# Reading the up projection's weight tiles with a step of 1, 2, 4 and 8 columns

## The chip, the cores and the metric

The kernel runs on one core of a Trainium2 chip. The metric is the time on the device in microseconds (us) of one execution; the times shown are medians of several runs. TensorE (PE in the profile) multiplies matrices: a weight load (PEld) puts the stationary operand, up to 128x128, into the array, and a matmul then streams the moving operand through it, column by column, into a bank of PSUM. VectorE (DVE), ScalarE (ACT) and the DMA queues of SyncE (SP) prepare operands beside it.

## What is computed

Two transformer blocks over 256 tokens with 2048 features, one after the other: the first with a gated linear recurrence, the second with three branches (pooling, convolution, sparse attention) and an MLP. The change touches the first product of that MLP only:

```python
h = rmsnorm(x, g[2])
m = jnp.square(jax.nn.relu(h @ w_up[l])) @ w_down[l]
x = x + rmsnorm(m, g[3])
```

`w_up` is 2048 x 8192, `w_down` is 8192 x 2048, all in fp32.

## The kernel before

Every fp32 product is made of three products of parts: an operand is split into a high part (rounded to the matrix unit's fp32r) and a low part (the rest), and high x high, high x low and low x high are summed in PSUM.

Weights come as a stream of chunks of 128 x 2048 numbers (1 MB), in the order of their use, built in the list `chunks`. `_pack` on the host lays them out; `_kchunks` makes of the matrix chunks that hold, for four blocks of 128 input rows, four tiles of 128 columns each, tile behind tile. `Stream.load` (L59) transfers a chunk into one of three buffers `wraw` on SyncE's queue. A chunk is split in two pieces of 1024 columns: `split_hi` (L87, ScalarE) writes the high part `whi`, `split_lo` (L98, VectorE) writes the low part `wlo` and, when the piece is the chunk's last, issues the next transfer. There are five buffers each of `whi` and `wlo`, so the split runs ahead of the matmuls.

The MLP is worked in four quarters, `q` = 0 to 3 (L1558). In each, the up projection computes 2048 of the 8192 hidden features for all 256 tokens: four groups of four output tiles (`Wide(4)`, one PSUM bank for each tile), each over 16 blocks of input features; then the down projection takes these 2048 features in (`Tok`, lines L409 to L411, where the weights are the moving operand). `full` (L453) calls `linear` for four chunks in turn, and `linear` (L430) takes a split piece and issues for each of its eight tiles the matmuls of `Wide.mac`: the tile of `whi` as stationary operand against 512 moving columns (high and low parts of 256 tokens, L376), and the tile of `wlo` against 256 moving columns (the high parts, L377). That makes 4 x 16 x 4 = 256 pairs of matmuls in a quarter, each matmul with a weight load of its own. After each piece `pumped` issues the next split and whatever vector or scalar work is due. The moving operand is `N`, the split and normalised input of the MLP, which stays in SBUF for all quarters. The tile of `whi` that a matmul takes is 128 columns that stand next to each other.

Of the kernel before, what the change touches and what calls it, by code (L numbers as in the profile page):

```python
# [23 lines left out]
P = 128  # L24
T = 256
D = 2048
KT = D // P
# [14 lines left out]
    _NV += _w  # L42

_POOL_FIX = 16
_ATT_GROUPS = 5


class Stream:
# [159 lines left out]
def tile_kernel(ctx: ExitStack, tc: tile.TileContext, d):  # L208
# [213 lines left out]
    def pumped(tiles):  # L422
        l = ws.split_lo()
        h = ws.split_hi()
        us = tiles * 0.3275
        S.pump(us, ACT=0.95 * h, DVE=1.13 * l, PE=us - 0.7)

    def linear(grp, kts, rhs, pieces, last_kt, before=None):

        kts = list(kts)  # L430
        per = len(kts) // pieces
        for p in range(pieces):
            hi, lo = ws.take()
            for a in range(per):
                kt = kts[p * per + a]
                x = rhs(kt)
                if isinstance(grp, Tok):
                    c = slice(a * 512, (a + 1) * 512)
                    for t in range(2):
                        grp.mac(t, hi[:, c], lo[:, c], *x[:2], kt == last_kt)  # L440
                    continue
                if isinstance(grp, Wide):
                    x = (x[2],)
                else:
                    x = x[:2]
                for m in range(grp.n):
                    c = (a * grp.n + m) * P
                    grp.mac(m, hi[:, c:c + P], lo[:, c:c + P], *x, kt == last_kt)
            if before is not None:
                before(kts[p * per])  # L450
            pumped(per * grp.n)

    def full(grp, rhs, n=KT):  # L453
        for c in range(n // 4):
            linear(grp, range(4 * c, 4 * c + 4), rhs, 2, n - 1)

    def full_by_bank(grp, rhs, evac, n=KT):

# [20 lines left out]
    def hl16(n):  # L479
        return sb.tile([P, 2, KT, T], F32R, tag="B32", bufs=2, name=n)  # L480
# [314 lines left out]
    for m in range(4):  # L795
        grp = Group(4)
# [14 lines left out]
        grp = Group(4)  # L811
# [20 lines left out]
    def out_last(rhs, fill=(None, None), idle=(0, 0)):  # L832

        grp = Group(4)
        sq = []

        def evac(b):
            if b == 0:
                sq.append(t4(n="sq"))
            act.activation(sq[0][:, 2 * b:2 * b + 2, :], grp.banks[b], AF.Square)  # L840
            if b == 0:
                norm.fold2(sq[0])

        full_by_bank(grp, rhs, evac)
        pumped(8)
        if fill[0]:
            fill[0]()
        t = norm.rstd(extra=[sq[0][:, 2, :], sq[0][:, 3, :]],
                      fill=(lambda: pumped(8), fill[1]) if fill[1] else (), idle=idle)
        S.free(T4=1)  # L850
        return grp, t
# [27 lines left out]
    def proj(n, half=None):  # L879
        if n not in pgrp:  # L880
            pgrp[n] = (Group(4), ws.take())
        grp, (hi, lo) = pgrp[n]
        for k in (0, 1) if half is None else (half,):
            for m in range(4):
                c = (4 * k + m) * P
                grp.mac(m, hi[:, c:c + P], lo[:, c:c + P], ph[:, k, :], pl[:, k, :], k == 1)
# [13 lines left out]
    g, r_copy = out_last(rhsY, fill=(lambda: proj(0, 0), lambda: proj(0, 1)))  # L900
# [55 lines left out]
    for n in range(4):  # L956
        g = Wide(4)
# [55 lines left out]
    for c in range(4):  # L1013
        for p in range(2):
            hi, lo = ws.take()
# [241 lines left out]
    for n in range(2):  # L1257
        g = Group(4)
# [71 lines left out]
    for m in range(8):  # L1330
        g = Group(3)
# [113 lines left out]
    for n in range(4):  # L1445
        if n == 3:
            A(1.28, lambda: table(AF.Sqrt))
            g, r_copy = out_last(rhsM, idle=(3, 7))
            break
        g = Wide(4)  # L1450
# [39 lines left out]
    rhsN = rhs_of(N, n_ready)  # L1490
# [67 lines left out]
    for q in range(4):  # L1558
        HD = hl16(f"HD{q}")
        ready = {}  # L1560
        for n in range(4):
            g = Wide(4)
            full(g, rhsN)
            if r4_done[0] is None:
                A(1.28, lambda: table(AF.Sqrt))
                r4_done[0] = norm.rstd(wait=False)
            up_done(n, g, HD, ready)
        if q == 0:
            for n in range(4):
                turn(n)  # L1570
        if q == 2:
            gains_ready.append(A(0.1, load_gains, take=T4[2]))
        rh = rhs_of(HD, ready)
        for n in range(4):
            if q == 3 and n == 3:
                break
            g = Tok()
            full(g, rh)
            down_done(q, n, g)
# [3 lines left out]
    g = Tok()  # L1583
# [24 lines left out]
    for t in range(2):  # L1608
        for a in range(4):
            hi, lo = hl[a // 2]  # L1610
            c = slice(a % 2 * 512, (a % 2 + 1) * 512)
# [6 lines left out]
def _kchunks(w, groups, kper=4):  # L1618

    k = w.shape[0] // P  # L1620
    out = []
    for cols in groups:
        a = np.concatenate([w[:, c:c + P] for c in cols], axis=1)
        a = a.reshape(k // kper, kper, P, len(cols) * P).transpose(0, 2, 1, 3)
        out.append(a.reshape(k // kper, P, kper * len(cols) * P))
    return np.ascontiguousarray(np.concatenate(out, axis=0))


def _fours(m, base=0):
    return [[base + (4 * g + i) * P for i in range(4)] for g in range(m // (4 * P))]  # L1630

# [7 lines left out]
def _cols(v):  # L1639
    return v.reshape(-1, P).T  # L1640
# [9 lines left out]
def _pack(i):  # L1650
    a = {}
    x, pe_ = i["x"][0], i["p"][0, 0]
    a["xT"] = _featT(x)
    a["pT"] = _featT(pe_)
    g = i["norm_gains_2"][0]
    vecs = [i["norm_pre"][0], i["norm_post"][0], i["a_conv_w"][0].reshape(-1), i["a_conv_b"][0],
            i["a_b_r"][0].reshape(-1), i["a_b_i"][0].reshape(-1), i["a_lam"][0], g[0], g[1], g[2], g[3],
            i["pool_scale_2"][0], i["conv_w_2"][0].reshape(-1)]
    a["vec"] = np.ascontiguousarray(np.concatenate([_cols(v) for v in vecs], axis=1))

    w = i["a_w_in"][0]
    order = []
    for m in range(4):
        order += [[(4 * m + t) * P for t in range(4)], [D + (4 * m + t) * P for t in range(4)]]
    a["a_in"] = _kchunks(w, order)
    ri = np.concatenate([i["a_w_r"][0], i["a_w_i"][0]], axis=2)
    ri = ri.reshape(4, 2, 2, P, 512).transpose(0, 3, 1, 2, 4)
    a["a_ri"] = np.ascontiguousarray(ri.reshape(4, P, 2048))
    a["a_out"] = _kchunks(i["a_w_out"][0], _fours(D))
    w = i["ple_w_proj"][0].reshape(2, P, 2, 2, 512).transpose(2, 1, 3, 0, 4)  # L1670
    a["ple_proj"] = np.ascontiguousarray(w.reshape(2, P, 2048))
    a["ple_gate"] = _kchunks(i["ple_w_gate"][0], _fours(D))

    w = i["w_in_2"][0]
    o_pool, o_u, o_c, o_b, o_q, o_k, o_v, o_qi, o_ki, o_wi = np.cumsum(
        [0, 1024, 1024, 1024, 1024, 1024, 256, 256, 1024, 64]).tolist()
    ki2 = np.concatenate([w[:, o_ki:o_ki + 64]] * 2, axis=1)
    att = np.concatenate([ki2, w[:, o_qi:o_qi + 1024], w[:, o_k:o_k + 256], w[:, o_q:o_q + 1024]], axis=1)
    a["att"] = _kchunks(att, _fours(2048))
    a["att3"] = _kchunks(att, [[16 * P, 17 * P, 18 * P]])  # L1680
    vw = np.concatenate([w[:, o_v:o_v + 256], w[:, o_wi:o_wi + 16]], axis=1)
    vw = vw.reshape(4, 4, P, 272).transpose(0, 2, 1, 3)
    a["vwi"] = np.ascontiguousarray(vw.reshape(4, P, 4 * 272))
    a["pool_in"] = _kchunks(w, _fours(1024, o_pool))
    pw = i["pool_w_2"][0].reshape(4, 2, P, 256).transpose(2, 0, 1, 3)
    a["pool_w"] = np.ascontiguousarray(pw.reshape(1, P, 2048))
    a["conv_in"] = _kchunks(w, [[o_u + m * P, o_c + m * P, o_b + m * P] for m in range(8)])
    a["gate"] = _kchunks(i["w_gate_2"][0], _fours(3 * D))
    a["branch"] = np.concatenate([_kchunks(i["w_branch_2"][0, n], _fours(D)) for n in range(3)])
    a["w_out"] = _kchunks(i["w_out_2"][0], _fours(D))  # L1690
    a["up"] = _kchunks(i["w_up_2"][0], _fours(4 * D))
    w = i["w_down_2"][0]
    a["down"] = np.concatenate([_kchunks(w[q * D:(q + 1) * D], _fours(D)) for q in range(4)])

    t = np.arange(_POOL_FIX)
    fix = np.concatenate([w_ / np.minimum(t + 1, w_) for w_ in (2, 4, 8, 16)])
    tri = np.where(np.arange(P)[None, :] <= np.arange(P)[:, None], 0.0, FLT_MASKED)
    a["cst"] = np.concatenate([np.broadcast_to(fix, (P, 4 * _POOL_FIX)), np.eye(P), tri],
                              axis=1).astype(np.float32)
    rel = i["rel_bias_2"][_bucket(P + np.arange(P)[:, None] - np.arange(T)[None, :])]  # L1700
    a["rel"] = np.ascontiguousarray(rel.reshape(P, T, 2, 4).transpose(2, 0, 3, 1))
    a["bg"] = np.ascontiguousarray(i["b_gate_2"][0].reshape(1, 3 * D))
    a["g3"] = np.ascontiguousarray(g[3].reshape(1, D))
    return a
# [18 lines left out]
```

## Time and profile before

| | |
|---|---|
| median of 3 runs | 1979.76 us (1979.06 to 1980.12) |
| the profiled execution, its own time | 1979.06 us |
| its span, first to last instruction | 1976.9 us |
| PE busy | 1956.2 us (99%) |
| PE weight loads busy | 1747.6 us (88%) |
| VectorE busy | 1227.7 us (62%) |
| ScalarE busy | 970.5 us (49%) |
| matmuls of L376 and L377 on the MLP's input `N` | 1024 each |

A busy time of PE is the time in which at least one matmul is under way. Matmuls overlap, so the length of one row is longer than the distance from its start to the next one's start; that distance (the pitch) is what adds up to the span. The span is 2.2 us shorter than the time of the same execution; a run's time differs from the median by at most 0.7 us.

### The profile page before, as it was taken

What the parts mean: (1) busy time and instruction counts of PE and PEld (TensorE: products, weight loads), DVE (VectorE), ACT (ScalarE), POOL (GpSimd) and SP (SyncE); (2) the same over time, 40 slices, a digit from 0 to 9 for tenths busy, and PEclk for the clock granted to TensorE, in tenths of its full rate; (3) what the DMA queues carried; (4) which work ended last, traced back from release to release, by engine and by line L of the source; (5) the groups of instructions that cost most, each with busy time, mean ns of one, the idle gap of its engine ahead of it and who ended that gap; (6) DMA issues with size and microseconds to landing.
All of it is one profiled execution on the core that took longest, in us unless ns stands there. A gap on an engine that the chain in (4) does not pass through costs nothing.

```text
span 1976.9 us, 28532 instructions
## 1 busy us (share of the span) xinstructions
PE 1956.2 (99%) x11865; PEld 1747.6 (88%) x11865; DVE 1227.7 (62%) x1503; ACT 970.5 (49%) x1200; POOL 0.3 (0%) x6
## 2 busy tenths in 40 slices
PE   9999999999999999999999999999999999999997
PEld 8999999899999998888888889788888888888886
DVE  6788857765587775455655555864456545645555
ACT  6576755653334444444444445555445435434542
POOL 0000000000000000000000000000000000000000
PEclk9999999999999999999999999999999999999999
DMA  7545464554445555555555555355555555555552
GB/s 282 179 172 186 171 216 170 193 191 157 146 170 178 174 181 197 197 204 199 200 206 192 197 192 179 147 192 173 194 187 192 192 192 192 207 197 183 183 192 103
DMA packets 56002, 368.49 MB, mean 186 GB/s; under 512 B 6208, under 2 KB 6464, under 8 KB 16448
## 3 DMA queue, kind: packets, MB, share of 16 engines
q1 hardware_dynamic: 53136, 361.16, 52.3%
q10 hardware_dynamic: 2736, 5.51, 0.9%
q8 instruction: 93, 1.52, 0.3%
q14 instruction: 37, 0.30, 0.0%
HBM read 364.54 MB, written 2.10 MB: 185 GB/s over the span
## 4 chain that ended last, share of the span: by engine, by line
PE 97%; DVE 1%; ACT 0%; DMA 0%; issue 0%; SPq 0%; DVEq 0%; ACTq 0%
PE ps L356 32%; PE ps L376 17%; PE ps L410 12%; PE ps L411 12%; PE ps L409 12%; PE ps L377 9%; PE ps L1052 0%; DMA wraw<-in_a_in 0%; PE ps L1121 0%; DVE X L1604 0%; PE ps L1021 0%; PE ps L1022 0%; PE ps L1023 0%; PE ps L1520 0%; DVE X L858 0%
## 5 line engine op out<-in xcount | busy, mean ns | idle before, releaser
L98 DVE TENSOR_TENSOR wlo<-wraw,whi 128x1024 fp32r<-128x1024 f32 (+2 forms) x701 | 832.0, 1191 | 666.8 <-ACT whi L87 665.8
L87 ACT ACTIVATE whi<-wraw 128x1024 fp32r<-128x1024 f32 (+2 forms) x701 | 722.4, 1033 | 938.9 <-PE ps L411 403.3
L376 PE MATMUL ps<-N,whi 128*128 128x512 f32 x1024 | 362.9, 399 | 3.4 <-DVE N L504 3.4
L356 PE MATMUL ps<-G,whi 128*128 128x256 f32 x1632 | 297.6, 285 | 0.0
L377 PE MATMUL ps<-N,wlo 128*128 128x256 f32 x1024 | 287.7, 281 | 0.0
L356 PEld LDWEIGHTS ps<-G,whi 128*128 128x128 f32 x1632 | 254.3, 192 | 1.9
L376 PEld LDWEIGHTS ps<-N,whi 128*128 128x128 f32 x1024 | 193.2, 189 | 51.9 <-DVE N L504 2.9
L356 PE MATMUL ps<-G,wlo 128*128 128x256 f32 x816 | 230.8, 283 | 0.0
L409 PE MATMUL ps<-whi,HD 128*128 128x512 f32 x512 | 199.4, 389 | 0.0
L410 PE MATMUL ps<-wlo,HD 128*128 128x512 f32 x512 | 199.2, 389 | 0.0
L411 PE MATMUL ps<-whi,HD 128*128 128x512 f32 x512 | 199.2, 389 | 0.0
L377 PEld LDWEIGHTS ps<-N,wlo 128*128 128x128 f32 x1024 | 194.0, 189 | 0.1
L356 PE MATMUL ps<-U,whi 128*128 128x256 f32 x1024 | 186.7, 285 | 1.6 <-DVE U L504 0.8
L356 PEld LDWEIGHTS ps<-U,whi 128*128 128x128 f32 x1024 | 160.8, 193 | 3.3 <-ACT whi L117 1.6
L356 PEld LDWEIGHTS ps<-G,wlo 128*128 128x128 f32 x816 | 156.4, 192 | 0.0
L409 PE MATMUL ps<-whi,G 128*128 128x512 f32 x384 | 149.7, 390 | 0.0
L411 PE MATMUL ps<-whi,G 128*128 128x512 f32 x384 | 149.4, 389 | 0.0
L410 PE MATMUL ps<-wlo,G 128*128 128x512 f32 x384 | 149.4, 389 | 0.0
L356 PE MATMUL ps<-U,wlo 128*128 128x256 f32 x512 | 145.6, 284 | 0.0
L409 PEld LDWEIGHTS ps<-whi,HD 128*128 128x128 f32 x512 | 96.1, 188 | 20.0
L411 PEld LDWEIGHTS ps<-whi,HD 128*128 128x128 f32 x512 | 96.1, 188 | 20.0
L410 PEld LDWEIGHTS ps<-wlo,HD 128*128 128x128 f32 x512 | 96.1, 188 | 19.7
(263 smaller groups left out, 2476.3 us busy)
## 6 DMA issues: line engine op xcount, KB each, us to landing
wraw<-in_up SPq DMA_DIRECT2D x64, 1024.0 KB, 4.8
wraw<-in_down SPq DMA_DIRECT2D x64, 1024.0 KB, 4.7
wraw<-in_gate SPq DMA_DIRECT2D x48, 1024.0 KB, 4.7
wraw<-in_a_in SPq DMA_DIRECT2D x29, 1024.0 KB, 4.8
wraw<-in_conv_in SPq DMA_DIRECT2D x32, 768.0 KB, 4.2
wraw<-in_branch SPq DMA_DIRECT2D x24, 1024.0 KB, 4.7
wraw<-in_a_out SPq DMA_DIRECT2D x16, 1024.0 KB, 4.8
wraw<-in_ple_gate SPq DMA_DIRECT2D x16, 1024.0 KB, 4.8
```

The source lines that it names most:

```text
L87: self.nc.scalar.activation(hi[:, :w], src, AF.Copy)
L98: self.nc.vector.tensor_tensor(lo, src, hi.bitcast(F32), op=ALU.subtract)
L356: pe.matmul(self.ps(m), lhsT, rhs, start=b not in self.begun, stop=stop, skip_group_check=True)
L376: pe.matmul(self.banks[m], wh, xhl, start=m not in self.begun, stop=False, skip_group_check=True)
L377: pe.matmul(self.banks[m][:, 0, :], wl, xhl[:, 0, :], start=False, stop=stop, skip_group_check=True)
L409: pe.matmul(o, xh[:, ts], wh, start=t not in self.begun, stop=False)
L410: pe.matmul(o, xh[:, ts], wl, start=False, stop=False)
L411: pe.matmul(o, xl[:, ts], wh, start=False, stop=stop)
```

## The change

For each quarter there is a number in `_UP_ORDER`: 1, 2, 4, 8. On the host, `_interleave` takes that many neighbouring weight tiles of the up projection and weaves their columns: column 0 of each, then column 1 of each, and so on. On the chip, a tile is then every second, fourth or eighth column of a stretch of 2, 4 or 8 x 128 columns (`tile_of`), so that its weight load reads the 128 columns with a step of 2, 4 or 8 numbers (8, 16 or 32 bytes). Quarter 0 keeps the step 1, and all other products too. The constant `_ATT_GROUPS`, which nothing reads, goes. The sequence of instructions on every engine is the same row for row.

```diff
-_ATT_GROUPS = 5
+_UP_ORDER = (1, 2, 4, 8)
...
+    def tile_of(w, i, r):
+
+        return w[:, i // r * r * P + i % r:(i // r + 1) * r * P:r]
+
-    def linear(grp, kts, rhs, pieces, last_kt, before=None):
+    def linear(grp, kts, rhs, pieces, last_kt, before=None, order=1):
...
                 for m in range(grp.n):
-                    c = (a * grp.n + m) * P
-                    grp.mac(m, hi[:, c:c + P], lo[:, c:c + P], *x, kt == last_kt)
+                    grp.mac(m, tile_of(hi, a * grp.n + m, order), tile_of(lo, a * grp.n + m, order), *x, kt == last_kt)
...
-    def full(grp, rhs, n=KT):
+    def full(grp, rhs, n=KT, order=1):
         for c in range(n // 4):
-            linear(grp, range(4 * c, 4 * c + 4), rhs, 2, n - 1)
+            linear(grp, range(4 * c, 4 * c + 4), rhs, 2, n - 1, order=order)
...
             g = Wide(4)
-            full(g, rhsN)
+            full(g, rhsN, order=_UP_ORDER[q])
...
+def _interleave(w, r):
+
+    n, p, c = w.shape
+    return np.ascontiguousarray(w.reshape(n, p, c // (r * P), r, P).transpose(0, 1, 2, 4, 3).reshape(n, p, c))
...
-    a["up"] = _kchunks(i["w_up_2"][0], _fours(4 * D))
+    w = _kchunks(i["w_up_2"][0], _fours(4 * D))
+    a["up"] = np.concatenate([_interleave(w[16 * q:16 * q + 16], _UP_ORDER[q]) for q in range(4)])
```

## Rows read from the trace of the kernel before

**Rows 1.** The page: busy time of PE and loads; granted clock in 40 slices.

```profile
PE 1956.2 (99%) x11865; PEld 1747.6 (88%) x11865; DVE 1227.7 (62%) x1503; ACT 970.5 (49%) x1200; POOL 0.3 (0%) x6
...
PEclk9999999999999999999999999999999999999999
```

**Rows 2.** The page: the chain that ended last, its shares of the span by engine.

```profile
PE 97%; DVE 1%; ACT 0%; DMA 0%; issue 0%; SPq 0%; DVEq 0%; ACTq 0%
```

**Rows 3.** The page's groups: line, engine, operands, count | busy us, mean ns | idle before.

```profile
L376 PE MATMUL ps<-N,whi 128*128 128x512 f32 x1024 | 362.9, 399 | 3.4 <-DVE N L504 3.4
...
L377 PE MATMUL ps<-N,wlo 128*128 128x256 f32 x1024 | 287.7, 281 | 0.0
```

**Rows 4.** Stretches of the up projection, quarters 0 to 3, columns as the head says.

```profile
core 0: us, PE busy (x) PEld busy (x) DVE busy (x) ACT busy (x) POOL busy (x), PEclk, DMA share, GB/s
...
1246.20:1340.80 94.60, 92.25 (x519) 80.06 (x520) 70.76 (x91) 53.65 (x75) 0.00 (x0) 0.98 0.51 178
1431.40:1521.90 90.50, 90.50 (x514) 78.50 (x513) 50.02 (x50) 43.87 (x52) 0.00 (x0) 1.00 0.53 186
1608.90:1699.40 90.50, 90.50 (x514) 78.54 (x513) 51.21 (x52) 42.90 (x50) 0.00 (x0) 1.00 0.54 186
1786.40:1876.90 90.50, 90.50 (x514) 78.45 (x513) 51.22 (x52) 42.90 (x50) 0.00 (x0) 1.00 0.53 186
```

**Rows 5.** Timeline in quarter 1: start us, us, engine, line, operands.

```profile
1500.16 0.28 PE L377 MATMUL ps<-N,wlo 128*128 128x256 f32 x1
1500.16 0.19 PEld L376 LDWEIGHTS ps<-N,whi 128*128 128x128 f32 x1
1500.28 0.40 PE L376 MATMUL ps<-N,whi 128*128 128x512 f32 x1
1500.28 0.19 PEld L377 LDWEIGHTS ps<-N,wlo 128*128 128x128 f32 x1
...
1500.52 0.28 PE L377 MATMUL ps<-N,wlo 128*128 128x256 f32 x1
1500.52 0.19 PEld L376 LDWEIGHTS ps<-N,whi 128*128 128x128 f32 x1
1500.63 0.40 PE L376 MATMUL ps<-N,whi 128*128 128x512 f32 x1
...
1500.86 0.28 PE L377 MATMUL ps<-N,wlo 128*128 128x256 f32 x1
```

**Rows 6.** Timeline in quarter 0 at the lower clock, with that stretch's window.

```profile
1255.40:1261.50 6.10, 6.10 (x28) 5.27 (x27) 6.07 (x7) 5.36 (x12) 0.00 (x0) 0.72 0.00 0
...
1256.32 0.63 PE L376 MATMUL ps<-N,whi 128*128 128x512 f32 x1
1256.32 0.33 PEld L377 LDWEIGHTS ps<-N,wlo 128*128 128x128 f32 x1
...
1256.74 0.41 PE L377 MATMUL ps<-N,wlo 128*128 128x256 f32 x1
1256.75 0.33 PEld L376 LDWEIGHTS ps<-N,whi 128*128 128x128 f32 x1
...
1256.96 0.63 PE L376 MATMUL ps<-N,whi 128*128 128x512 f32 x1
```

**Rows 7.** Timeline: eight loads with one moving column each, and the next matmul.

```profile
1240.93 0.97 PEld L564 LDWEIGHTS ps<-one,sq 128*128 128x128 f32 x8 [0.43 <-ACT sq L840]
1240.93 1.05 PE L564 MATMUL ps<-one,sq 128*128 128x1 f32 x8 [0.35 <-ACT sq L840]
...
1241.85 0.81 PE L336 MATMUL ps<-zero 128*128 128x512 bf16 x3
```

**Rows 8.** The page's DMA issues of the up projection: count, KB each, us to landing.

```profile
wraw<-in_up SPq DMA_DIRECT2D x64, 1024.0 KB, 4.8
```

**Rows 9.** Groups in quarter 1 (1431.4 to 1521.9): the splits and the loads.

```profile
L377 PEld LDWEIGHTS ps<-N,wlo 128*128 128x128 f32 x256 | 48.4, 189 | 0.0
...
L98 DVE TENSOR_TENSOR wlo<-wraw,whi 128x1024 fp32r<-128x1024 f32 x32 | 39.2, 1224 | 37.6 <-ACT whi L87 37.6
L87 ACT ACTIVATE whi<-wraw 128x1024 fp32r<-128x1024 f32 x32 | 33.9, 1059 | 46.2 <-PE ps L376 44.6 <-PE ps L411 1.7
```

**Rows 10.** Groups of weight loads: transposes of contiguous tiles, and of one repeated column.

```profile
L1520 PEld LDWEIGHTS ps<-cst,X 128*128 128x128 f32 x32 | 3.6, 140 | 0.5
...
L591 PEld LDWEIGHTS ps<-cst,c 128*128 128x128 f32 x10 | 1.2, 134 | 1.1 <-DVE c L586 1.0
```

## The prediction

> **What bounds the kernel now.** I read the page's busy times and chain first. TensorE is busy for 99% of the span, its clock stands at nine tenths or more in all 40 slices [rows 1], and the chain of work that ended last is PE for 97% [rows 2]. So only a change in the time from one matmul to the next can move the end by much; all that the vector and scalar engines do beside it is cover. Next I looked at the lines that the change touches, L376 and L377: 1024 matmuls each with a 128x512 and a 128x256 moving operand [rows 3], in four quarters of 256 pairs. The stretches of quarters 1, 2 and 3 (counting from 0) last 90.5 us each, all of it PE busy at full clock; quarter 0, at 94.6 us, holds some start-up waits and a short stretch at a lower clock, and its loads stay as they are [rows 4]. So a pair takes 90.5 / 256 = 353.5 ns, and the three quarters that change take 271.5 us of the 1976.9.
>
> The timeline shows how a pair is made [rows 5]. The matmul with 256 columns holds the engine for 0.12 or 0.11 us, about 117 ns, and the one with 512 for 0.24 or 0.23 us, about 236 ns. The row's own length (0.28, 0.40) is not the pitch, since matmuls are pipelined. A weight load starts together with the matmul before the one it serves: the load for L376 runs under the short matmul of L377, the load for L377 under the long one of L376. So a load has 117 ns of cover on one side and 236 ns on the other.
>
> Is the short slot set by its 256 columns or by the load under it? Two places tell. Where the granted clock fell to its lower level, 1.2 GHz, after a wait of PE, a pair takes 0.64 us (1256.32 to 1256.96) for 768 columns, 0.833 ns each [rows 6], one a cycle; at 2.4 GHz that is 107 ns for 256 columns, and the slot of 117 has some 10 ns on top. And where eight weight loads come behind one another with one moving column each, they take from 1240.93 to 1241.85, 0.92 / 8 = 115 ns per load [rows 7]. So the short slot is as long as a contiguous load allows, within 2 ns: a load that gets slower shows there at once, and one that gets faster gains nothing.
>
> **The change part by part.** The instructions are the same, row for row, on all engines: no instruction, wait or transfer is added or moved, and what differs on the chip is the step between the 128 columns that a load reads: 4 bytes before, and 8, 16 and 32 bytes in quarters 1, 2 and 3.
>
> The transfers of in_up stay 1024 KB each, 64 of them [rows 8], from an array of the same shape; the interleaving is host work, outside the time. The splits (L87, L98) read and write whole pieces contiguously as before. They take 33.9 and 39.2 us of the 90.5 of a quarter, and most of ScalarE's idle time ahead of L87 is waiting for PE [rows 9]. A slower PE only makes their cover larger, and none of them becomes late. The tile a matmul waits for is the same whole piece in both kernels, so no matmul waits for more than before. These parts cost nothing.
>
> What is left is 768 pairs, each with two strided loads. The trace has no load with a step above one column, so its price must be bounded.
>
> From below: the moving side still needs its 107 + 10 ns, so at most 117 - 115 = 2 ns a pair could be gained, 1.5 us in 768 pairs, under 0.1%. The nearest load with another step is that of L591, which reads one column 128 times (step 0): 134 ns, where the loads of the ordinary transposes of L1520 take 140 [rows 10]. So a step that isn't one has no price of its own; but step 0 never leaves its place and doesn't show what spreading out costs. Lower end: no cost.
>
> From above: the longest loads in the trace are the ones in the stretch at the lower clock, 0.33 us where the same loads otherwise take 0.19 [rows 5, 6]. If a strided load were longer by as much, some 143 ns (0.33 us against the 189 ns that is the mean in quarter 1 [rows 9]), the short slot would go to 117 + 143 = 260 ns, and the long slot, whose load would need 115 + 143 = 258, would grow by 22: 165 ns a pair.
>
> Between them I go by how fast addresses advance. A moving operand takes a column of 4 bytes every 0.417 ns, 16 bytes in 1.7 ns. A contiguous load takes a column in about (115 - 10) / 128 = 0.82 ns. With a step of 8 bytes it covers 16 bytes in 1.64 ns, no faster than the moving operand is read all the time; I take it as free. With 16 and 32 bytes it would have to cover ground two and four times as fast as any read by TensorE in this trace. I take it that each column then costs one more access time, that is twice the 105 ns: 210 + 10 = 220 ns. In the short slot that adds 220 - 117 = 103 ns; under the long slot 220 is still below 236, so that the cover there holds, with 16 ns left. If the price per column is half as large, the load takes 167 ns and adds 50.
>
> The Trainium skill, page "Advanced Engine Details and Errata", section "Memory Cachelines", says that SBUF has lines of 16 bytes, that two hits on a line are needed to hide the latency, and that an access to another line each time is penalised; it gives no price for TensorE. By that rule the step of 8 bytes (two columns a line) is free and those of 16 and 32 bytes (one column a line) are not; no row of this trace can show it. The page "TensorE: Matmul & The Clock Gate", section "LDWEIGHTS (loading the stationary operand)", gives columns / 1.2 ns, 107 ns here, where the row gives 115 with all overheads; with 107 added per load the sum would be 512 x (107 + 107 + 10 - 117) = 55 us instead of the one below.
>
> Sum: quarters 2 and 3 hold 2 x 256 = 512 pairs; 512 x 103 ns = 52.7 us. The profiled execution took 1979.06 us (span 1976.9 and 2.2 around it), so 2031.8; the median of the runs shown is 0.7 higher, so I say 2032.
>
> **The rivals.**
> *No change.* TensorE gets a moving column in half the time that a load takes per column (0.417 against 0.82 ns). If the memory serves an access per column whatever its address, a load has twice the time it needs at any step, and nothing changes: 1979 to 1980. For it speaks that the load time follows the engine's own clock (0.19 to 0.33 when the clock halves [rows 5, 6]), as if the array and not the memory set it. Against it: both rates are of contiguous reads.
> *A step of 8 bytes pays as well.* If a load reads every fp32 column in two passes at the moving rate, its addresses advance twice as fast as I reckoned, and quarter 1 pays too: 768 x 103 = 79 us, 2058.
> *Only the step of 32 bytes pays*, if reads of neighbouring 16 bytes overlap and only skipped ones collide: 256 x 103 = 26 us, 2006.
> *A gain* is bounded by the 2 ns a pair above; for more, the long slot's 236 - 213 = 23 ns beyond its columns would have to come from collisions of the two reads that a stride avoids: up to 768 x 23 = 18 us. No row speaks for it.
> *The clock falls*, since columns move for a smaller part of the time: 320 of 456 ns instead of 320 of 353. It fell in quarter 0 only behind a wait of PE, so this is unlikely; a pair would be two slots of twice the low-clock load, 427 each: 854 ns, and the kernel beyond 2200.
>
> **How the numbers follow.** Forecast (16 and 32 bytes pay) 0.44; no change 0.33; 8 bytes too 0.12; only 32 bytes 0.06; gain 0.03; clock 0.02. A measurement of this kernel tells a difference of about 0.2% (4 us) from none; the chances are 0.64 slower, 0.33 the same, 0.03 faster. The forecast's own range goes from half the price, 512 x 50 = 26 us (2005), to the upper bound, 512 x 165 = 84 us (2064). To hold the time 8 times in 10 the whole range must take in no change with 2 us of scatter, so its low end is 1977; its high end, 2064, takes in the case of three quarters (2058).
>
> **What the profile would show.** If I am right, the quarters' stretches become about 94.6, 90.5, 117 and 117 us; L377's matmul keeps the engine for 0.22 us in the last two, L376's load there lasts longer than 0.19 by about 0.1 us and L376's matmul still follows 0.23 later; the down projections keep their times; ScalarE waits longer ahead of L87. If all four quarters keep their times, the step that fails is the access time per column. If quarter 1 grows, it is the reckoning by 16 bytes. If the long slot grows too, the cover of 16 ns was too small. If quarters 2 and 3 differ, the price depends on the step itself and not only on leaving the 16 bytes.

## The result and the profile after

The changed kernel takes 2043.38 us (median of 4 runs, 2042.56 to 2044.43), the kernel before 1979.94 us (4 runs): 1.032 times as long, 95% interval 1.0308 to 1.0332, or 63.4 us more. The forecast was slower, 2032 us, 52.7 us more, in a range of 1977 to 2064.

The page of the changed kernel answers to [rows 1]: PE is busy for the same 99%, at the same clock, for 65 us longer. So TensorE did not wait for another engine; its own instructions got slower.

```profile
span 2041.6 us, 28532 instructions
...
PE 2021.0 (99%) x11865; PEld 1838.8 (90%) x11865; DVE 1228.5 (60%) x1503; ACT 972.4 (48%) x1200; POOL 0.3 (0%) x6
...
PEclk9999999999999999999999999999999999999998
```

The stretches of the four up projections, as [rows 4], and behind them two of the down projections between them (which took 87.0 us each before):

```profile
core 0: us, PE busy (x) PEld busy (x) DVE busy (x) ACT busy (x) POOL busy (x), PEclk, DMA share, GB/s
1247.10:1341.80 94.70, 92.15 (x519) 80.06 (x520) 70.86 (x92) 53.70 (x75) 0.00 (x0) 0.98 0.50 178
1432.20:1523.00 90.80, 90.80 (x515) 80.99 (x514) 50.02 (x51) 43.98 (x53) 0.00 (x0) 1.00 0.52 186
1609.80:1730.30 120.50, 120.50 (x515) 120.50 (x514) 51.63 (x52) 43.33 (x51) 0.00 (x0) 1.00 0.40 141
1817.00:1941.70 124.70, 124.70 (x515) 124.67 (x514) 51.79 (x53) 43.37 (x51) 0.00 (x0) 1.00 0.39 136
1523.00:1609.80 86.80, 86.80 (x385) 71.81 (x384) 46.41 (x44) 36.95 (x38) 0.00 (x0) 1.00 0.55 194
1730.30:1817.00 86.70, 86.70 (x384) 71.78 (x383) 46.35 (x44) 36.97 (x38) 0.00 (x0) 1.00 0.58 205
```

Quarters 0 (step 1) and 1 (step 2) keep their times, quarters 2 (step 4) and 3 (step 8) take some 30 and 34 us more, and nothing else changes. A window's edges are mine; the sharper measure is from the first to the last start of L376's 256 matmuls. The view of one line gives count: shortest/median/longest ns, first to last start. These are L376's matmuls and then its loads in quarters 1, 2 and 3:

```profile
L376 PE MATMUL ps<-N,whi x256: 392/397/404, 1432.4 to 1522.5; 128*128 128x512 f32 x128
L376 PE MATMUL ps<-N,whi x256: 401/512/517, 1610.0 to 1729.7; 128*128 128x512 f32 x128
L376 PE MATMUL ps<-N,whi x256: 406/520/530, 1817.3 to 1941.1; 128*128 128x512 f32 x128
...
L376 PEld LDWEIGHTS ps<-N,whi x256: 193/196/198, 1432.2 to 1522.4; 128*128 128x128 f32 x128
L376 PEld LDWEIGHTS ps<-N,whi x256: 308/310/311, 1609.8 to 1729.6; 128*128 128x128 f32 x128
L376 PEld LDWEIGHTS ps<-N,whi x256: 316/327/335, 1817.0 to 1940.9; 128*128 128x128 f32 x128
```

That is 90.1, 119.7 and 123.8 us, or, divided by the 255 steps between 256 starts, 353, 469 and 485 ns a pair. The two slow quarters bring 29.6 + 33.7 = 63.3 us, which is the difference of the medians (of the 65 us between the two profiled executions, some 1 us lies ahead of the up projection). The forecast had 456 ns for both. From here on a quarter's time is this one, from first to last start; before it was 90.1 us in quarters 1, 2 and 3, here quarter 2:

```profile
L376 PE MATMUL ps<-N,whi x256: 389/398/403, 1608.9 to 1699.0; 128*128 128x512 f32 x128
```

The timeline in quarter 2, beside [rows 5], shows the new rhythm:

```profile
1690.12 0.28 PE L377 MATMUL ps<-N,wlo 128*128 128x256 f32 x1
1690.24 0.51 PE L376 MATMUL ps<-N,whi 128*128 128x512 f32 x1
1690.59 0.28 PE L377 MATMUL ps<-N,wlo 128*128 128x256 f32 x1
1690.71 0.51 PE L376 MATMUL ps<-N,whi 128*128 128x512 f32 x1
...
1690.12 0.31 PEld L376 LDWEIGHTS ps<-N,whi 128*128 128x128 f32 x1
1690.33 0.34 PEld L377 LDWEIGHTS ps<-N,wlo 128*128 128x128 f32 x1
1690.59 0.31 PEld L376 LDWEIGHTS ps<-N,whi 128*128 128x128 f32 x1
```

The short matmul still seems to hold the engine for 0.12 us; the long one's row starts at its old place and has become 0.51 instead of 0.40 us. But its load (1690.12) is not over when that row starts (1690.24), and the next load starts only at 1690.33. So, as the profile records them, a matmul's row may begin while its weights are still on their way; the wait for the load is inside the row of the matmul that needs it, and not ahead of it.

### The profile page after: what moved, and what is told of

It is laid out like the page before. It is cut to its first block, busy times and chain, and to the rows that moved or that the text cites. A ratio compares the mean times of both kernels' runs of the same rounds, so it can differ in the third digit from the quotient of the medians.

```text
span 2041.6 us, 28532 instructions
## 1 busy us (share of the span) xinstructions
PE 2021.0 (99%) x11865; PEld 1838.8 (90%) x11865; DVE 1228.5 (60%) x1503; ACT 972.4 (48%) x1200; POOL 0.3 (0%) x6
## 4 chain that ended last, share of the span: by engine, by line
PE 98%; DVE 1%; ACT 0%; DMA 0%; issue 0%; SPq 0%; DVEq 0%; ACTq 0%
PE ps L356 31%; PE ps L376 20%; PE ps L409 12%; PE ps L410 12%; PE ps L411 12%; PE ps L377 9%; PE ps L1055 0%; DMA wraw<-in_a_in 0%; PE ps L1124 0%; DVE X L1607 0%; PE ps L1024 0%; PE ps L1025 0%; PE ps L1026 0%; PE ps L1523 0%; DVE X L861 0%
## 5 line engine op out<-in xcount | busy, mean ns | idle before, releaser
L87 ACT ACTIVATE whi<-wraw 128x1024 fp32r<-128x1024 f32 (+2 forms) x701 | 723.5, 1034 | 1001.7 <-PE ps L411 401.3
L376 PE MATMUL ps<-N,whi 128*128 128x512 f32 x1024 | 426.4, 458 | 3.5 <-DVE N L507 3.5
L377 PE MATMUL ps<-N,wlo 128*128 128x256 f32 x1024 | 290.6, 284 | 0.0
L376 PEld LDWEIGHTS ps<-N,whi 128*128 128x128 f32 x1024 | 262.1, 256 | 25.8 <-DVE N L507 2.9
L377 PEld LDWEIGHTS ps<-N,wlo 128*128 128x128 f32 x1024 | 272.5, 266 | 0.0
```

The costliest lines, as they stand in the source:

```text
L87: self.nc.scalar.activation(hi[:, :w], src, AF.Copy)
L376: pe.matmul(self.banks[m], wh, xhl, start=m not in self.begun, stop=False, skip_group_check=True)
L377: pe.matmul(self.banks[m][:, 0, :], wl, xhl[:, 0, :], start=False, stop=stop, skip_group_check=True)
```

## What had to be told apart

The kind of the loss is clear from this; its size is not: 116 and 132 ns a pair instead of 103. Two theories:

- **A.** A strided load takes longer by itself than I reckoned, about 235 ns at step 4 and 243 at step 8 (half of 469 and 485), with or without a matmul beside it.
- **B.** A load takes the 220 ns of the prediction, but a strided load and a stream of 512 moving columns slow each other, so that the long slot grows from 236 to 250 and 266.

All edits below are made on the changed kernel. Each of these kernels but the last was run once, and what is read from it is the time of its quarters in the trace.

## Experiment 1: only one of the two loads strided

```diff
-grp.mac(m, tile_of(hi, a * grp.n + m, order), tile_of(lo, a * grp.n + m, order), *x, kt == last_kt)
+grp.mac(m, tile_of(hi, a * grp.n + m, order), tile_of(lo, a * grp.n + m, 1), *x, kt == last_kt)
```

> Only the loads of L376 (under the matmul with 256 columns) keep their step of 1, 2, 4, 8; the loads of L377 read contiguous columns of the woven array, that is, other columns than the product needs. Theory A (a strided load itself takes longer than I took, about 235 ns at step 4 and 243 at step 8, with or without a matmul beside it): a pair is 235 + 236 = 471 ns in quarter 2 (120.6 us) and 243 + 236 = 479 in quarter 3 (122.6 us). Theory B (a strided load takes 220 ns as in the prediction, but slows the matmul of 512 columns that streams beside it to 250 and 266): 220 + 236 = 456 in both, 116.7 us each. Quarter 1 stays at 90.5 in both.

Measured: 2040.64 us beside 1979.18 for the kernel before on the same chip. The lines are quarters 2 and 3 of L376:

```profile
L376 PE MATMUL ps<-N,whi x256: 393/509/509, 1611.7 to 1729.7; 128*128 128x512 f32 x128
L376 PE MATMUL ps<-N,whi x256: 408/517/528, 1817.2 to 1938.0; 128*128 128x512 f32 x128
```

118.0 and 120.8 us, 463 and 474 ns a pair.

The other way round, with the step on `lo` and none on `hi`:

> Only the loads of L377 (under the matmul with 512 columns) keep their step of 1, 2, 4, 8; the loads of L376 read contiguous columns of the woven array, other columns than the product needs. Theory A (load 235 and 243 by itself): the cover of 236 holds it but for 7 ns: quarter 2 stays at 90.5 us, quarter 3 goes to 92. Theory B (strided load and 512 streaming columns slow each other): long slot 250 and 266, quarter 2 goes to 94 us and quarter 3 to 98.

Measured: 1980.83 us beside 1979.18. Quarters 2 and 3 of L376, then of L377's loads:

```profile
L376 PE MATMUL ps<-N,whi x256: 395/398/398, 1607.9 to 1698.0; 128*128 128x512 f32 x128
L376 PE MATMUL ps<-N,whi x256: 389/403/404, 1785.4 to 1878.3; 128*128 128x512 f32 x128
...
L377 PEld LDWEIGHTS ps<-N,wlo x256: 308/308/311, 1607.9 to 1698.0; 128*128 128x128 f32 x128
L377 PEld LDWEIGHTS ps<-N,wlo x256: 316/320/327, 1785.4 to 1878.3; 128*128 128x128 f32 x128
```

90.1 and 92.9 us, 353 and 364 ns a pair. These loads are recorded as 120 and 132 ns longer than contiguous ones, and, against the kernel before, 256 of them at step 4 cost nothing, 256 at step 8 cost 11 ns each. So the price is almost all paid under the matmul with 256 columns, as forecast. Theory B expected 94 and 98 us here and falls; A expected 90.5 and 92.

In the run before, A expected 120.6 and 122.6; it came out 2.6 and 1.8 us under that, between A and B in quarter 2, but with a difference between the quarters, which only A has. So that half alone does not decide. Added up, the two halves give at step 8 what both loads together cost (120 + 11 = 131 of 132 ns), at step 4 a little less (109 + 0 of 116). These 7 ns, some 2 us in the whole kernel, stay open.

The pair without a price is not the same in these two runs, though. Quarter 1 of the one just shown, with contiguous loads for L376 and a step of 2 for L377:

```profile
L376 PE MATMUL ps<-N,whi x256: 392/392/392, 1432.1 to 1520.5; 128*128 128x512 f32 x128
```

That is 88.4 us, 347 ns a pair where the kernel before has 353; in quarter 1 of the run before it is 89.3 us, 350 ns. So 353 ns is not a floor, and what moves it was not tested. Counted from the same run's quarter 1, L377's loads cost 7 ns at step 4 and 18 at step 8, and L376's 113 and 124. A small part of theory B, which asked for 14 and 30 ns under the 512 columns, is therefore not ruled out, and the 7 ns that stay open may be of the same kind.

## Experiment 2: the load's own time

With 256 moving columns in both matmuls of a pair, any load above 117 ns shows its own length.

```diff
+            g.short = True
...
-            pe.matmul(self.banks[m], wh, xhl, start=m not in self.begun, stop=False, skip_group_check=True)
+            if m not in self.begun or not self.short:
+                pe.matmul(self.banks[m], wh, xhl, start=m not in self.begun, stop=False, skip_group_check=True)
+            else:
+                pe.matmul(self.banks[m][:, 0, :], wh, xhl[:, 0, :], start=False, stop=False, skip_group_check=True)
```

> Both loads strided as in the changed kernel, but in the up projection both matmuls of a pair have 256 columns (the product of high weights with the low part of the input is left out, except for the first input block). A slot is then the longer of 117 ns of matmul and the load. Theory A: 2 x 117 = 234 ns a pair in quarters 0 and 1 (60 us), 2 x 235 = 470 in quarter 2 (120 us), 2 x 243 = 486 in quarter 3 (124 us), that is, the same as with 512 columns. Theory B: 2 x 220 = 440 (113 us) in both quarters.

Measured: 1995.69 us. The timeline in quarter 2 (step 4), then quarter 3 (step 8); in this kernel L380 is the matmul with high weights and L381 the one with low weights:

```profile
1619.65 0.40 PE L381 MATMUL ps<-N,wlo 128*128 128x256 f32 x1
1619.88 0.40 PE L380 MATMUL ps<-N,whi 128*128 128x256 f32 x1
...
1621.29 0.40 PE L380 MATMUL ps<-N,whi 128*128 128x256 f32 x1
...
1849.78 0.40 PE L381 MATMUL ps<-N,wlo 128*128 128x256 f32 x1
1850.02 0.40 PE L380 MATMUL ps<-N,whi 128*128 128x256 f32 x1
...
1851.47 0.40 PE L380 MATMUL ps<-N,whi 128*128 128x256 f32 x1
```

Seven slots from 1619.65 to 1621.29 and from 1849.78 to 1851.47: 234 and 241 ns each, where quarter 1 (step 2) has 119 and quarter 0 (contiguous) 121. A pair is 468 and 482, as much as with 512 columns in the long matmul, though a third fewer columns are moved. Theory A is confirmed with its numbers: the load alone sets the pace, and it takes 234 ns at step 4 and 241 at step 8. A contiguous load took 115 by the reckoning with [rows 7], which goes from the first matmul's start to the start of the next line's. From load to load it is a little less. In two narrow windows of that place, each row holds the two loads then under way, the first and second and the seventh and eighth of the eight:

```profile
1240.93 0.30 PEld L564 LDWEIGHTS ps<-one,sq 128*128 128x128 f32 x2 [0.43 <-ACT sq L840]
...
1241.60 0.30 PEld L564 LDWEIGHTS ps<-one,sq 128*128 128x128 f32 x2
```

Six steps in 0.67 us are 112 ns a load.

## Experiment 3: cover for both loads

```diff
+            g.long = True
...
-            pe.matmul(self.banks[m][:, 0, :], wl, xhl[:, 0, :], start=False, stop=stop, skip_group_check=True)
+            pe.matmul(self.banks[m], wl, xhl, start=False, stop=stop, skip_group_check=True)
```

> Both loads strided as in the changed kernel, but both matmuls of a pair have 512 columns (the product of low with low parts is added). Contiguous, a pair is 2 x 236 = 472 ns, 121 us in quarters 0 and 1. Theory A: 2 x 236 = 472 in quarter 2 (121 us), 2 x 243 = 486 in quarter 3 (124 us). Theory B: 2 x 250 = 500 (128 us) and 2 x 266 = 532 (136 us).

Measured: 2098.76 us, which includes 256 more moving columns in each of 1024 pairs. In this kernel L377 is the matmul with high weights; quarters 1, 2 and 3:

```profile
L377 PE MATMUL ps<-N,whi x256: 394/394/394, 1457.3 to 1576.3; 128*128 128x512 f32 x128
L377 PE MATMUL ps<-N,whi x256: 400/400/401, 1663.8 to 1783.7; 128*128 128x512 f32 x128
L377 PE MATMUL ps<-N,whi x256: 396/408/413, 1871.2 to 1996.0; 128*128 128x512 f32 x128
```

119.0, 119.9 and 124.8 us, slots of 233, 235 and 245 ns. Under 512 moving columns a load with step 4 costs 2 ns; one with step 8, 11 ns. That is near A again (121, 121, 124), and not B (128 and 136 in the last two). But at step 8 the slot of 245 is longer than the load's own 241, so 4 ns of it come from the two running together or from something else; the runs don't tell.

## Experiment 4: which steps pay

Experiment 2 with steps of 3, 5, 6 and 7 columns on an array that is not woven:

```diff
-_UP_ORDER = (1, 2, 4, 8)
+_UP_ORDER = (3, 5, 6, 7)
...
-        return w[:, i // r * r * P + i % r:(i // r + 1) * r * P:r]
+        s = i % (1024 - 127 * r)
+        return w[:, s:s + 127 * r + 1:r]
```

> As in the run with two matmuls of 256 columns in a pair (whose slots show the load itself: 233 ns at step 4, 241 at step 8), but the weight array is not woven and the loads read with steps of 3, 5, 6 and 7 columns (12, 20, 24 and 28 bytes) in quarters 0 to 3; they take other columns than the product needs. Theory L1 (a place of 16 bytes costs two column times, which two columns in it hide): at step 3, columns lie 2, 1, 1 in three places of 16 bytes, 6 column times for 4 columns, 1.5 times 115 = about 173 ns a slot (some 89 us in quarter 0); 233 at steps 5, 6, 7, 119 us each. Theory L2 (only steps of 16 bytes and more pay): 117 ns at step 3 (63 us plus waits in quarter 0), 233 at the others. Theory L3 (whatever leaves 8 bytes pays in full): 233 already at step 3 (119 us). What step 8 has above step 4 (8 ns): if it grows with the step, 235, 237 and 239 ns at steps 5, 6, 7.

Quarter 0 (step 3) in the timeline, eight slots, and one slot of quarter 1 (step 5):

```profile
1331.77 0.34 PE L380 MATMUL ps<-N,whi 128*128 128x256 f32 x1
1331.94 0.34 PE L381 MATMUL ps<-N,wlo 128*128 128x256 f32 x1
...
1333.18 0.33 PE L380 MATMUL ps<-N,whi 128*128 128x256 f32 x1
...
1499.81 0.40 PE L381 MATMUL ps<-N,wlo 128*128 128x256 f32 x1
1500.04 0.38 PE L380 MATMUL ps<-N,whi 128*128 128x256 f32 x1
...
1501.17 0.39 PE L381 MATMUL ps<-N,wlo 128*128 128x256 f32 x1
```

Step 3 takes (1333.18 - 1331.77) / 8 = 176 ns, step 5 takes (1501.17 - 1499.81) / 6 = 227. Quarters 1, 2 and 3 (steps 5, 6, 7) end after 115.6, 116.0 and 119.1 us by L381's starts, where experiment 2 had 119.0 at step 4 and 123.0 at step 8. So L1 holds: 173 were expected at step 3, one and a half times the contiguous load; L2 (117) and L3 (233) fall. A place of 16 bytes costs two column times; two columns in it hide that. Another wording fits these steps as well: a load covers at most 8 bytes in a column time, and no column takes more than two. Telling them apart would need pairs of neighbouring columns far from each other, which no run has. The Trainium skill, page "Advanced Engine Details and Errata", section "Memory Cachelines", says that SBUF has lines of 16 bytes, that at least two hits on a line are needed to absorb the access latency, and that a different line at each access is penalised; it gives no price. These runs agree with it for an fp32 load, at 0.9 ns a column with two or more in 16 bytes and 1.8 with one. The moving operand in experiment 5 does not keep to it: with two columns in 16 bytes it already takes 0.89 ns a column instead of 0.46.

Beyond step 4 the time doesn't grow evenly with the step: 234, 227, 227, some 234, 241 at steps 4 to 8, where 235, 237 and 239 were the expectation for a growing one at 5, 6 and 7. The runs don't say why.

## Experiment 5: the moving operand with a step

The prediction's reckoning took the moving operand's 16 bytes in 1.7 ns as the pace that a load can be read at. If one limit of the memory stood behind both, a stepped moving operand would pay by the same rule. All loads are contiguous here, and L376 and L377 read `N` with steps of 1, 2, 4 and 8 columns:

```diff
-                    x = (x[2],)
+                    x = (x[2] if order == 1 else apart(x[3], kt, order),)
...
+    def apart(h, k, r):
+        s = min(k * T, KT * T - r * T)
+        return h.rearrange("p a k t -> p a (k t)")[:, :, s:s + 255 * r + 1:r]
```

> All loads contiguous; instead the moving operand N is read with a step of 1, 2, 4, 8 columns in quarters 0 to 3 (other columns of N than the product needs; the weight array is not woven). If the limit is the time for a place of 16 bytes (233 / 128 = 1.82 ns) and the moving side has the same: step 2 puts two columns in it, 0.91 ns each where it takes 0.42 now: slots of 233 and 466 ns, a pair 700, 179 us in quarter 1; steps 4 and 8 one column each, 466 and 932, 358 us in quarters 2 and 3. If the moving side isn't bound by places: 90.5 us in every quarter.

Measured: 2229.17 us. Quarters 1, 2 and 3:

```profile
L376 PE MATMUL ps<-N,whi x256: 615/637/637, 1433.4 to 1608.4; 128*128 128x512 f32 x128
L376 PE MATMUL ps<-N,whi x256: 622/641/642, 1696.2 to 1873.0; 128*128 128x512 f32 x128
L376 PE MATMUL ps<-N,whi x256: 593/611/611, 1960.8 to 2126.2; 128*128 128x512 f32 x128
```

175.0, 176.8 and 165.4 us: 0.89, 0.90 and 0.84 ns for each of 768 columns. Contiguous, the same measure gives 353 / 768 = 0.46. Step 2 met the expectation for a common limit (179 us), steps 4 and 8 did not come near it (358), and no quarter stayed at the 90.5 us of the other case. The moving operand pays once for not being contiguous, some twice the time per column, and then nothing more, up to step 8. At step 8 it takes a new place of 16 bytes every 0.84 ns; a load at the same step takes one every 241 / 128 = 1.9 ns. So the 1.8 ns are a limit of the load and not of every read of that memory.

## Experiment 6: the step or the place in the program

```diff
-_UP_ORDER = (1, 2, 4, 8)
+_UP_ORDER = (8, 4, 2, 1)
```

> The steps are 8, 4, 2, 1 in quarters 0 to 3, on the array woven so. If the price goes with the step alone: quarters of 94.6 + 34 = 128, 120, 90.5, 90.5 us, and 2043 us in all. If it goes with the place in the program (quarter 3 costs more than 2 for another reason than its step): the last quarter is again the longest above its step's due.

Measured: 2041.32 us. Quarters 0 to 3 of L376:

```profile
L376 PE MATMUL ps<-N,whi x256: 513/520/634, 1247.5 to 1372.5; 128*128 128x512 f32 x128
L376 PE MATMUL ps<-N,whi x256: 401/512/517, 1463.7 to 1583.5; 128*128 128x512 f32 x128
L376 PE MATMUL ps<-N,whi x256: 392/397/404, 1671.0 to 1761.1; 128*128 128x512 f32 x128
L376 PE MATMUL ps<-N,whi x256: 389/398/403, 1848.6 to 1938.7; 128*128 128x512 f32 x128
```

The price went with the steps: 119.8 us at step 4 in quarter 1 and 90.1 at steps 2 and 1. Step 8 in quarter 0 costs 31 us (125.0 against 94.0) instead of 34. The longer pairs leave out a wait there: PE was idle ahead of L376 for `N` for 3.4 us before [rows 3] and is for 1.1 here. The stretch at the lower clock behind that wait [rows 6] is gone with it (granted clock 1.00 from 1256 to 1264 us). That is 2.3 us and, estimated from some five pairs that took 0.64 instead of 0.35 us, 1.4 more, enough for the difference.

And step 2 in all four quarters, `_UP_ORDER = (2, 2, 2, 2)`:

> Step 2 in all four quarters. By the trace of the changed kernel (quarter 1 as before, loads recorded 8 ns longer) step 2 is free: 1980 us, ratio 1.000 within 0.002. If each load costs 8 ns that show in the slot of 256 columns, 1024 x 6 ns = 6 us, ratio 1.003.

Measured: 1981.39 us against 1981.31 on the same chip, ratio 0.9999, 95% interval 0.9989 to 1.0008. At the 6 ns in each short slot that were expected in the other case, the ratio would be 1.003, outside the interval. Step 2 is free; the 8 ns by which such a load's row is longer never reach the pace.

## Why the prediction was right, and where it wasn't

**What bounds the kernel** was right: PE, at full clock, and in these quarters the pair. Nothing outside the pairs changed: the down projections stay within 0.3 us of before, and ScalarE only waits longer for PE. Its idle time ahead of L87 in quarter 2, against 46.2 us in [rows 9]:

```profile
L87 ACT ACTIVATE whi<-wraw 128x1024 fp32r<-128x1024 f32 x33 | 35.0, 1062 | 78.4 <-PE ps L376 74.2 <-DVE dacc L1550 2.5 <-PE ps L411 1.7
```

**Where the cover is** was right: next to none under the short matmul, which took nearly the whole price, and enough under the long one for a step of 4 (lo_only at 90.1 us). My 2 ns under the short one are 5 by the 112 ns from load to load. The 16 ns that I thought were left under the long one were 2: the load takes 234 of 236 ns, and at step 8 it is out of cover.

**Step 2 free, steps 4 and 8 paying** was right. The rivals *no change* and *8 bytes pays as well* fall by quarters 2 and 1, *only 32 bytes* by quarter 2, the clock by its 1.00 in all three windows. *A gain* falls for this kernel, whose quarter 1 kept its 90.1 us; that the pair can be shorter than 353 ns is seen only in experiment 1, by up to 7 ns.

**The term that was mis-sized** is the price of a strided load: 103 ns a pair forecast, 116 and 132 measured. I had taken 10 ns off the 115 of a contiguous load as a fixed part and doubled the other 105, for 220. Experiment 2 gives 234, which is all of the 115 doubled and 4 ns more (10 more than twice 112; these stay open). Those 10 ns come from the matmul's slot, 117 against the 107 of its columns; nothing said that a load has such a part. With 2 x 115 the short slot adds 113 and the sum is 512 x 113 = 58 us. What is left of the 63.3 is nearly all step 8: 7 ns more for each load (241), and the long slot out of cover by 11, of which 241 - 236 explains 5. Quarters 2 and 3 apart was the prediction's sign of a price that depends on the step itself; it came up, with 4 us between them.

**The reason given for twice the time** held in its result and not in its ground. That a load's price goes by places of 16 bytes fits every step tried (experiment 4). That it is because the memory can't be read faster is not: the moving operand reads separate places at 0.84 ns (experiment 5), so the pace it has when contiguous, on which I built, was no measure for the load. The rival *no change* rested on the same thing, an access per column at any address; the moving side has it beyond step 2, and the load does not.

**Where it shows in the trace** I had wrong: I expected L377's matmul to keep the engine for 0.22 us. Its pitch is 0.12 as before; the wait is in L376's row, which begins before its load has ended.

## What to carry to other kernels

In these runs an fp32 weight load reads with a step of two columns at no cost and takes about twice as long from a step of four on, 227 to 241 ns instead of 115; whether that is seen depends on the moving operand of the matmul before it, since 512 columns (some 236 ns) hide a load at step 4 and 256 columns (117) hide none of its extra time. So for each strided load look up which matmul stands ahead of it. When costing something that gets slower by a factor, take a fixed part off only if a row of that same instruction shows it, and don't take one port's pace as the measure for another.

## What the runs showed of the hardware

- The slot of a load under 256 moving columns, by step: 121 ns contiguous and 119 at step 2, where the columns alone need some 117; then the load's own time, 176 at step 3, 234 at 4, 227 at 5 and 6, 241 at 8.
- A moving fp32r operand with a step of 2 takes 0.89 ns a column instead of 0.46, and 0.84 at step 8: it has no tolerance for step 2, where the load has, and doesn't get worse beyond.
- Pairs whose loads cost nothing took from 347 to 353 ns (88.4 to 90.1 us in quarter 1, by the run); why is open.
- A matmul's row can begin before its weight load has ended: 1690.24 against a load from 1690.12 that lasts 0.31 us. A longer load is then seen in the length of the row and not as a gap.
